# Which queue issues three kinds of stores: az, the normalised z and the projected a, from ScalarE and not from SyncE

## The chip, the core and the metric

The kernel runs on one core of one Trainium2 chip. The metric is the device time of one execution in microseconds. A core has TensorE (PE in the rows; PEld is its weight load), VectorE (DVE), ScalarE (ACT), GpSimd (POOL) and SyncE (SP), which here only issues transfers. A name with a q, as SPq, is an engine's queue of issues.

## What is computed

One decoder layer over 4096 positions of 1024 channels, in float32:

```
h = LN(x)                                        # stored, needed again in unit 3
a_val, a_gate, a_z, b_u, b_v, b_z = split(h @ w_in)        # six of 512 channels
y_a = silu(LN(causal_conv31(a_val * sigmoid(a_gate)))) * silu(a_z)
y_b = gelu(b_u) * (tril(w_s) @ LN(gelu(b_v)) + b_s) * silu(b_z)
h = LN(alpha * h + concat(y_a, y_b) @ w_out)
out = h + sigmoid(h @ w_gate + b_gate) * (p @ w_ple)
```

The convolution is depthwise along the positions, so what it reads, a = a_val * sigmoid(a_gate), is needed with channels on the partitions.

## The kernel before

There are five matrix products with 1024 x 1024 weights, called units: 0 gives a, 1 gives u and v, 2 gives z of both branches (b_z and a_z), 3 is the output projection and 4 the gate. Each unit goes over 16 pairs of 128 positions (`NP`, index p), and for each pair `group` computes a 256 x 1024 product by Strassen-Winograd in seven products of 12 matmuls each (float32 as the sum of two fp32r halves, hi and lo, by three products). The seven go through the PSUM banks pb, pe, pa and pd: ScalarE or VectorE saves pb and pe to pa, s5 (s in the rows), u2 (u) and pd before the next product overwrites or reads them. Those are the evictions of lines 330 to 334. The left operands of the next pair are made meanwhile: `left` copies a tile to ahi on ScalarE and leaves the rest, alo, to VectorE or GpSimd.

Much goes through tensors in DRAM. In unit 0, `a_out` (line 519) transposes a pair's a into the tile at and stores it with four transfers (one for each 128 channels, line 535) to aD, which the convolution reads some pairs later. In unit 2, `body_c` takes silu of az in place and stores it (line 641) to azD; unit 3 loads it again as cz. In unit 3, `z_out` (line 706) normalises a pair's z with one ACTIVATE for each 128 positions (line 716) and stores it (line 717) to zT; unit 4 loads it as zr. Beside this, weights of the next unit are prepared: `combos` loads four quarters (bq, line 183), subtracts them on GpSimd (lines 187 to 196) and stores the seven operands to twD (lines 186 to 197); they come back as wst (line 414) near the end of a unit. Other transfers of this kind are qD (line 251, left operands kept for units 1 and 2, loaded again as qa and qb), hT (493), xr (465), uD, ybD, cD, and hr and y, loads for unit 3.

All transfers are issued by SyncE through the name `dma`. The order on each engine is not the order of the code: a scheduler places all instructions by its own estimate of times, and what an engine is given it runs in that order. Every transfer adds to one of eight semaphores, DMAHW0 to DMAHW7, which the scheduler hands out in turn; a transfer whose semaphore was last used by another waits until that one has landed. An instruction of an engine that waits holds those behind it.

Of the kernel before, what the change touches and what calls it, by code (L numbers as in the profile page):

```python
# [16 lines left out]
P = 128  # L17
# [47 lines left out]
def hybrid_layer_kernel(  # L65
# [16 lines left out]
):  # L82
    nc = tc.nc
    dma = nc.sync.dma_start
    act = nc.scalar.activation
    tt = nc.vector.tensor_tensor
    ptt = nc.gpsimd.tensor_tensor
# [11 lines left out]
    def big(shape, name, dt=F32):  # L99
        return pool.tile(shape, dt, tag="big", name=name, bufs=7)  # L100
# [4 lines left out]
    def utile(shape, name, dt=F32):  # L105
        return pool.tile(shape, dt, tag="u", name=name, bufs=7)
# [4 lines left out]
    def sbank(name):  # L111
        return pbank("S", name, 2)
# [17 lines left out]
    zT = [dram.tile([2, P, D], F32, name=f"zT{p}") for p in range(NP)]  # L130
    qD = [dram.tile([P, 7, C], F32, name=f"qD{p}") for p in range(NP)]
    aD = [dram.tile([CT, P, 2, SB // 2], F32, name=f"aD{b}") for b in range(NS)]
# [3 lines left out]
    azD = [dram.tile([2, P, C], F32, name=f"azD{p}") for p in range(NP)]  # L136
    twD = [None] + [dram.tile([7, P, 4, C], F32, name=f"twD{u}") for u in range(1, 5)]

    def pair(t):
        return t.rearrange("j p d -> p j d")  # L140
# [3 lines left out]
    def moments(halves, mv):  # L144
        st = pool.tile([P, 2, 6], F32, tag="st", name="st", bufs=4)
        for i, h in enumerate(halves):
            nc.vector.bn_stats(st[:, i, :], h)
        nc.vector.bn_aggr(mv, st[:, 0 : len(halves), :])

    def mvtile(n):  # L150
        t = pool.tile([P, 2, 2], F32, tag="mv", name="mv", bufs=6)
        return t[:, 0:n, :]
# [23 lines left out]
    def combos(u):  # L176


        for c in range(4):
            q = big([P, 4, C], "bq")  # L180
            for i in range(2):
                for j in range(2):
                    dma(q[:, 2 * i + j], wq[u, i, j][:, c])
            yield
            for n, k in ((1, 0), (2, 2), (3, 3)):
                dma(twD[u][ROW[n]][:, c], q[:, k])
            ptt(q[:, 0], q[:, 1], q[:, 0], op=SUB)
            dma(twD[u][ROW[5]][:, c], q[:, 0])
            yield
            ptt(q[:, 1], q[:, 3], q[:, 1], op=SUB)  # L190
            dma(twD[u][ROW[7]][:, c], q[:, 1])
            yield
            ptt(q[:, 3], q[:, 3], q[:, 0], op=SUB)
            dma(twD[u][ROW[6]][:, c], q[:, 3])
            yield
            ptt(q[:, 2], q[:, 2], q[:, 3], op=SUB)
            dma(twD[u][ROW[4]][:, c], q[:, 2])
            yield
# [166 lines left out]
    def conv(b, ct):  # L365

        n = SB // 2
        ca = pool.tile([P, 2, HALO + n], F32, tag="ca", name="ca", bufs=2)  # L370
        zy = pool.tile([P, HALO - 1 + n], F32, tag="zy", name="zy", bufs=1)
        if b == 0:
            nc.gpsimd.memset(ca[:, :, 0:HALO], 0.0)
        else:
            dma(ca[:, :, 0:HALO], aD[b - 1][ct][:, :, n - HALO :])
        dma(ca[:, :, HALO:], aD[b][ct])
        e, o = ca[:, 0], ca[:, 1]
        ptt(zy, e[:, 1:], o[:, 0 : HALO - 1 + n], op=SUB)  # L378
        ptt(e, e, o, op=SUB)
        even, odd = (pbank("acc", "acc", 2) for _ in range(2))  # L380
        for k in range(NE):
            w, src = cs_sb[:, ct, k : k + 1], o[:, k : k + n]
            if k == 0:
                nc.vector.tensor_scalar(even, src, w, cb_sb[:, ct : ct + 1], op0=MUL, op1=ADD)
            else:
                stt(even, src, w, even, op0=MUL, op1=ADD)  # L386
            yield
        for k in range(NE):
            if k < NE - 1:
                src = zy[:, k : k + n]  # L390
                dst = src if k == NE - 2 else odd
                stt(dst, src, cw_sb[:, ct, 2 * k + 1 : 2 * k + 2], odd if k else even, op0=MUL, op1=ADD)  # L392
                yield
            src = e[:, k : k + n]
            stt(  # L395
                src if k == NE - 1 else even, src, cw_sb[:, ct, 2 * k : 2 * k + 1], even,
                op0=MUL, op1=ADD,
            )
            yield
        for h, src in ((0, e[:, HALO:]), (1, zy[:, HALO - 1 :])):  # L400
            dma(cD[b][ct][:, :, h], src.rearrange("p (t m) -> p t m", m=P // 2))
        convolved.append((b, ct))
# [15 lines left out]
    def broadcast(src, n, name, tile_of=big):  # L418
        t = tile_of([P, n, src.shape[-1]], name)
        for i in range(n):  # L420
            dma(t[:, i], src[i : i + 1, :].partition_broadcast(P))
        return t
# [95 lines left out]
    def a_out(p, c):  # L518

        at = big([P, CT, 2, P], "at")  # L520
        for j in range(2):
            tp = sbank("ta")
            for ct in range(CT):
                nc.tensor.transpose(
                    out=tp[:, ct * P : (ct + 1) * P], in_=c[j][:, ct * P : (ct + 1) * P],
                    identity=ident,
                )
            act(
                at[:, :, :, j * 64 : (j + 1) * 64],
                tp.rearrange("p (c h m) -> p c h m", c=CT, h=2), ID,  # L530
            )
            yield
        t0 = (p % 4) * P
        for ct in range(CT):
            dma(aD[p // 4][ct][:, :, t0 : t0 + P], at[:, ct])
        if p % 4 == 3:
            for ct in range(CT):
                bg_conv.add(conv(p // 4, ct))
# [88 lines left out]
    def body_c(p, L, W, between):  # L627
        if p == 1:
            bg_w.add(combos(3))
        if p == NP - 3:  # L630
            for i in range(2):
                cgb.append(broadcast(crow[i : i + 1, :], 1, "cgb", utile))
            load_y(0)
        elif p >= NP - 2:
            bg_x.add(y_rows(p - NP + 2))
        ua = big([P, 2, 2, C], "ua")
        us, az = ua[:, 0], ua[:, 1]
        dma(us, pair(uD[p // 2][2 * (p % 2) : 2 * (p % 2) + 2]))
        pa, pd = group(L, W, None, az[:, 0], az[:, 1], between)
        act(az, az, AF.Silu)  # L640
        dma(pair(azD[p]), az)
        for j, ps in ((0, pa), (1, pd)):
            zz = utile([P, C], "zz")
            act(zz, ps, AF.Silu)
            ptt(us[:, j], us[:, j], zz, op=MUL)
        dma(pair(ybD[p]), us)
        if p == NP - 2:
            load_y(1)
        elif p == NP - 1:
            load_h(0)  # L650
            load_y(2)
# [3 lines left out]
    def load_y(p):  # L655
        b, q = p // 4, p % 4
        while (b, CT - 1) not in convolved:
            bg_conv.step(1)
        cz = big([P, 2, 2, C], "cz")
        dma(  # L660
            flat(cz[:, 0]).rearrange("p (c x) -> p c x", c=CT),
            cD[b][:, :, 2 * q : 2 * q + 2].rearrange("c p j h m -> p c (j h m)"),
        )
        dma(cz[:, 1], pair(azD[p]))
        CZ[p] = cz
        Y[p] = big([P, 2, D], "y")
        dma(Y[p][:, :, C:], pair(ybD[p]))

    def y_rows(p):
        cz, y = CZ.pop(p), Y[p]  # L670
        cc = flat(cz[:, 0]).rearrange("p (c j x) -> p c j x", c=CT, j=2)
        for j in (1, 0):
            tp = sbank("tc")
            for ct in range(CT):
                nc.tensor.transpose(
                    out=tp[:, ct * P : (ct + 1) * P],
                    in_=cc[:, ct, j],
                    identity=ident,
                )
            act(y[:, j, 0:C], tp, ID)  # L680
        yield
        mv = mvtile(2)
        for j in (1, 0):
            moments([y[:, j, 0:C]], mv[:, j, :])
        nb = scale_bias(mv)
        yield
        for j in (1, 0):
            ya = y[:, j, 0:C]
            act(ya, ya, ID, scale=mv[:, j, 1:2], bias=nb[:, j : j + 1])
            yield  # L690
            ptt(ya, ya, cgb[0][:, 0], op=MUL)
            ptt(ya, ya, cgb[1][:, 0], op=ADD)
            act(ya, ya, AF.Silu)
            ptt(ya, ya, cz[:, 1, j], op=MUL)
            yield
# [4 lines left out]
    def load_h(p):  # L700
        H[p] = big([P, 2, D], "hr")
        dma(H[p], pair(hT[p]))
# [4 lines left out]
    def z_out(p, z):  # L707
        mv = mvtile(2)
        for j in range(2):
            moments([z[:, j, 0:C], z[:, j, C:]], mv[:, j, :])  # L710
            yield
        nb = scale_bias(mv)
        yield
        yield
        for j in range(2):
            act(z[:, j], z[:, j], ID, scale=mv[:, j, 1:2], bias=nb[:, j : j + 1])
            dma(zT[p][j], z[:, j])
            yield

    def body_d(p, L, W, between):  # L720
# [168 lines left out]
```

## Time and profile before

| | us |
|---|---|
| median of 3 runs | 1897.69 |
| lowest and highest run | 1892.99, 1901.14 |
| the profiled execution | 1898.2 |
| its span, from first to last instruction | 1896.5 |
| TensorE busy in it | 1804.0 |
| VectorE | 1413.6 |
| GpSimd | 1269.9 |
| ScalarE | 892.4 |
| transfers of SyncE's queue, share of 16 DMA engines | 55.3% |

Durations below are from this one profiled execution. Times of day are us from the start of its span. A busy time is the union of an engine's instructions; issues of transfers are not counted as busy. Unit 0 runs to some 430 us, unit 1 to 770, unit 2 to 1080, unit 3 to 1470, unit 4 to the end.

### The profile page before, as it was taken

Reading aid. Unit: us, or ns where it says so; the run is one execution under the profiler, and the core shown is the slowest. Engines: PE = TensorE matmul, PEld = TensorE weight load, DVE = VectorE, ACT = ScalarE, POOL = GpSimd, SP = SyncE. Lnnn points to the kernel's source line nnn. Section 1 sums busy time; section 2 is a strip of 40 time slices with the busy share of each in tenths; the row PEclk is TensorE's granted clock in tenths of the full one; section 3 lists DMA queues with packets and bytes.
Section 4 is the critical chain, followed back from the end, with each engine's and each line's share of the span. In section 5 each row is a group of like instructions: output and inputs, shape, how many; then the busy total and the mean of one; then the engine's idle time right before and its main releaser. Section 6 shows DMA issues by size and latency. Waiting matters only on the chain. (4 is left out here: it accounts for less than half of the span.)

```text
span 1896.5 us, 24392 instructions
## 1 busy us (share of the span) xinstructions
PE 1804.0 (95%) x8322; PEld 1470.9 (78%) x8322; DVE 1413.6 (75%) x2176; ACT 892.4 (47%) x1438; POOL 1269.9 (67%) x1015
## 2 busy tenths in 40 slices
PE   4799999999999999999999899999999999999999
PEld 3687788877788887788888677787887787888887
DVE  8637877797787778978787998887558856665654
ACT  4655555565455555544444634445555422332222
POOL 2878987458777676588668568757676856655541
PEclk9899999999999999999999889999999999999999
DMA  6579776586734445898666758745555322222311
GB/s 239 195 236 359 248 235 206 194 287 211 239 124 147 139 142 173 302 358 298 211 198 227 272 186 284 242 150 191 197 189 220 119 95 78 89 90 95 100 54 52
DMA packets 184940, 363.62 MB, mean 192 GB/s; under 512 B 49648, under 2 KB 74224, under 8 KB 177136
## 3 DMA queue, kind: packets, MB, share of 16 engines
q1 hardware_dynamic: 184816, 362.07, 55.3%
q8 instruction: 66, 1.08, 0.2%
q14 instruction: 58, 0.48, 0.1%
HBM read 211.02 MB, written 150.99 MB: 191 GB/s over the span
## 5 line engine op out<-in xcount | busy, mean ns | idle before, releaser
L232 POOL TENSOR_TENSOR alo<-s,ahi 128x512 fp32r<-128x512 f32 x192 | 262.8, 1382 | 260.7 <-ACT ahi L231 252.9
L312 PE MATMUL pb<-whi,ahi 128*128 128x512 f32 x960 | 385.9, 402 | 18.3 <-ACT pa L330 5.2
L313 PE MATMUL pb<-wlo,ahi 128*128 128x512 f32 x960 | 378.4, 394 | 1.6 <-DVE wlo L173 1.6
L314 PE MATMUL pb<-whi,alo 128*128 128x512 f32 x960 | 378.4, 394 | 0.1
L312 PE MATMUL pe<-whi,ahi 128*128 128x512 f32 x640 | 258.9, 405 | 19.6 <-ACT ahi L231 8.5
L314 PE MATMUL pe<-whi,alo 128*128 128x512 f32 x640 | 256.6, 401 | 2.1 <-POOL alo L232 2.1
L313 PE MATMUL pe<-wlo,ahi 128*128 128x512 f32 x640 | 254.6, 398 | 4.2 <-DVE wlo L173 4.2
L312 PEld LDWEIGHTS pb<-whi,ahi 128*128 128x128 f32 x960 | 182.3, 190 | 63.6 <-ACT pa L330 8.8
L314 PEld LDWEIGHTS pb<-whi,alo 128*128 128x128 f32 x960 | 182.1, 190 | 39.5 <-POOL alo L232 0.6
L313 PEld LDWEIGHTS pb<-wlo,ahi 128*128 128x128 f32 x960 | 182.7, 190 | 38.4 <-DVE wlo L173 2.6
L232 POOL TENSOR_TENSOR alo<-qa,ahi 128x512 fp32r<-128x512 f32 x128 | 171.2, 1353 | 48.1 <-ACT ahi L231 47.8
L231 ACT ACTIVATE ahi<-s 128x512 fp32r<-128x512 f32 x192 | 119.7, 629 | 138.9 <-DVE s L284 54.6
L386 DVE SCALAR_TENSOR_TENSOR acc<-ca,cs_sb,acc 128x512 f32<-128x512 f32 x240 | 180.1, 750 | 4.3
L395 DVE SCALAR_TENSOR_TENSOR acc<-ca,cw_sb,acc 128x512 f32<-128x512 f32 x240 | 179.0, 746 | 0.1
L392 DVE SCALAR_TENSOR_TENSOR acc<-zy,cw_sb,acc 128x512 f32<-128x512 f32 x224 | 166.8, 745 | 1.2 <-POOL zy L378 0.4
L312 PEld LDWEIGHTS pe<-whi,ahi 128*128 128x128 f32 x640 | 122.7, 192 | 47.1 <-ACT ahi L231 10.3
L232 POOL TENSOR_TENSOR alo<-qb,ahi 128x512 fp32r<-128x512 f32 x96 | 126.8, 1329 | 39.2 <-ACT ahi L231 38.2
L313 PEld LDWEIGHTS pe<-wlo,ahi 128*128 128x128 f32 x640 | 122.6, 191 | 30.4 <-DVE wlo L173 6.5
L232 DVE TENSOR_TENSOR alo<-tp,ahi 128x512 fp32r<-128x512 f32 x144 | 98.2, 683 | 62.9 <-ACT ahi L231 60.5
L314 PEld LDWEIGHTS pe<-whi,alo 128*128 128x128 f32 x640 | 122.3, 191 | 27.8 <-POOL alo L232 3.3
L312 PE MATMUL pd<-whi,ahi 128*128 128x512 f32 x320 | 129.4, 404 | 4.4 <-ACT pd L330 3.2
L159 POOL TENSOR_TENSOR mv<-mv,nhalf 128x2 f32<-128x2 f32 (+1 forms) x81 | 55.2, 687 | 111.2 <-DVE mv L158 110.3
(151 smaller groups left out, 4006.7 us busy)
## 6 DMA issues: line engine op xcount, KB each, us to landing
qa<-qD SPq DMA_DIRECT2D x32, 1024.0 KB, 6.5
twD<-bq SPq DMA_DIRECT2D x112, 256.0 KB, 5.7
wst<-twD SPq DMA_DIRECT2D x28, 1024.0 KB, 6.9
qb<-qD SPq DMA_DIRECT2D x32, 768.0 KB, 6.8
xr<-in_x SPq DMA_DIRECT2D x32, 512.0 KB, 5.4
hT<-xr SPq DMA_DIRECT2D x32, 512.0 KB, 3.8
qD<-s SPq DMA_DIRECT2D x64, 256.0 KB, 2.9
bq<-in_wq SPq DMA_DIRECT2D x64, 256.0 KB, 5.2
```

Source lines behind the costliest of these rows:

```text
L159: ptt(mv[:, :, 1], mv[:, :, 1], nhalf[:, 0:n], op=ALU.pow)
L231: act(hi, src, ID)
L232: eng.tensor_tensor(lo, src, hi.bitcast(F32), op=SUB)
L312: nc.tensor.matmul(ps, lhsT=ah[:, k, :], rhs=wh[:, k, :], start=start and k == 0, stop=False, **kw)
L313: nc.tensor.matmul(ps, lhsT=ah[:, k, :], rhs=wl[:, k, :], start=False, stop=False, **kw)
L314: nc.tensor.matmul(ps, lhsT=al[:, k, :], rhs=wh[:, k, :], start=False, stop=k == 3, **kw)
L386: stt(even, src, w, even, op0=MUL, op1=ADD)
L392: stt(dst, src, cw_sb[:, ct, 2 * k + 1 : 2 * k + 2], odd if k else even, op0=MUL, op1=ADD)
L395: stt(src if k == NE - 1 else even, src, cw_sb[:, ct, 2 * k : 2 * k + 1], even, op0=MUL, op1=ADD,)
```

## The change

A second name, `dma_act`, issues from ScalarE's queue, and three of the stores use it. Nothing else in the code differs; the new line shifts all line numbers behind it by one.

```
+    dma_act = nc.scalar.dma_start
...
         for ct in range(CT):
-            dma(aD[p // 4][ct][:, :, t0 : t0 + P], at[:, ct])
+            dma_act(aD[p // 4][ct][:, :, t0 : t0 + P], at[:, ct])
...
         act(az, az, AF.Silu)
-        dma(pair(azD[p]), az)
+        dma_act(pair(azD[p]), az)
...
             act(z[:, j], z[:, j], ID, scale=mv[:, j, 1:2], bias=nb[:, j : j + 1])
-            dma(zT[p][j], z[:, j])
+            dma_act(zT[p][j], z[:, j])
```

The scheduler makes a new order of it. In units 1, 2 and 4 the engines' orders are nearly the same but for the moved stores; in units 0 and 3 all five differ. Three places, with the semaphores for which each row waits (a name of an engine there is that engine's own semaphore).

ScalarE in unit 0 at the third pair, behind the eviction u; c_1001 is the sigmoid of this pair's first half of the gate, s_1143 a left operand of the next pair. Before:

```order
L528 ACTIVATE at<-ta 128x8x64 [waits PE_49]
L549 ACTIVATE c_1001<-c_1001 128x512 [waits DMAHW4_49,DVE_49]
L262 ACTIVATE zq<-tp 128x512 [waits PE_49]
L231 ACTIVATE ahi<-tp 128x512 [waits Pool_49]
L231 ACTIVATE ahi<-s_1143 128x512 [waits DVE_49]
L231 ACTIVATE ahi<-s_1150 128x512 [waits DVE_49,PE_49,Activation_49]
L330 ACTIVATE pd<-pb 128x512 [waits PE_49]
```

and now:

```order
L529 ACTIVATE at<-ta 128x8x64 [waits PE_49]
L536 DMA aD_125<-at 256x1x128 [waits DMAHW5_49,Activation_49]
L263 ACTIVATE zq<-tp 128x512 [waits PE_49]
L232 ACTIVATE ahi<-tp 128x512
L536 DMA aD_125<-at 256x1x128 [waits DMAHW7_49]
L536 DMA aD_125<-at 256x1x128 [waits DMAHW1_49]
L536 DMA aD_125<-at 256x1x128 [waits DMAHW3_49]
L550 ACTIVATE c_1001<-c_1001 128x512 [waits DMAHW4_49,DVE_49]
L232 ACTIVATE ahi<-s_1143 128x512 [waits DVE_49]
L331 ACTIVATE pd<-pb 128x512 [waits PE_49]
```

The four stores of a now stand in ScalarE's order, one behind the second copy to at and three behind the ahi, and the sigmoid and the eviction pd stand behind them. At the fourth pair all four stand in a row behind the ahi, then one ahi and pd.

ScalarE in unit 2 at the second pair, around the store of az; zz is silu of b_z, s_7599 the eviction of pe in the next pair. Before:

```order
L640 ACTIVATE ua<-ua 128x1024 [waits DVE_49]
L644 ACTIVATE zz<-pd 128x512 [waits PE_49]
L330 ACTIVATE s_7599<-pe 128x512
L330 ACTIVATE pa<-pb 128x512 [waits PE_49,Activation_49]
L231 ACTIVATE ahi<-qa 128x512 [waits DMAHW5_49]
```

and now:

```order
L641 ACTIVATE ua<-ua 128x1024 [waits DVE_49]
L642 DMA azD_158<-ua 128x2x512 [waits DMAHW5_49,Activation_49]
L645 ACTIVATE zz<-pd 128x512 [waits PE_49]
L331 ACTIVATE s_7599<-pe 128x512
L331 ACTIVATE pa<-pb 128x512 [waits PE_49]
```

The store of az, whose semaphore was last used by the load of qa, stands between silu of az and zz, and the evictions s and pa behind it.

SyncE in unit 3 at the first pair, where the prepared weights, the loads of cz, y and hr and the stores of z (zT) meet. Before:

```order
L183 DMA bq<-in_wq 128x512 x4
L717 DMA zT_93<-z 128x1024
L660 DMA cz<-cD_130 128x4x256
L717 DMA zT_93<-z 128x1024
L664 DMA cz<-azD_161 128x2x512
L186 DMA twD_176<-bq 128x512 x3
L667 DMA y<-ybD_145 128x2x512
L702 DMA hr<-hT_80 128x2x1024
```

and now:

```order
L184 DMA bq<-in_wq 128x512 x4
L187 DMA twD_176<-bq 128x512
L661 DMA cz<-cD_130 128x4x256
L665 DMA cz<-azD_161 128x2x512
L187 DMA twD_176<-bq 128x512 x2
L668 DMA y<-ybD_145 128x2x512
L703 DMA hr<-hT_80 128x2x1024
```

The two stores of z are gone from SyncE, and the loads of cz do not stand behind them.

## Rows read from the trace of the kernel before

**Rows 1.** The page: each engine's busy us, share of the span, instructions.

```profile
PE 1804.0 (95%) x8322; PEld 1470.9 (78%) x8322; DVE 1413.6 (75%) x2176; ACT 892.4 (47%) x1438; POOL 1269.9 (67%) x1015
```

**Rows 2.** Stretches: length, busy PE, PEld, DVE, ACT, POOL; granted clock, DMA share, GB/s.

```profile
0.00:67.00 67.00, 32.98 (x104) 22.99 (x104) 57.06 (x71) 34.99 (x44) 28.94 (x29) 0.87 0.59 213
...
100.00:430.00 330.00, 321.04 (x1544) 262.44 (x1543) 249.45 (x390) 188.47 (x310) 236.20 (x170) 0.99 0.74 256
...
780.00:1050.00 270.00, 269.44 (x1201) 222.64 (x1200) 219.24 (x325) 123.83 (x211) 211.93 (x173) 1.00 0.79 267
1050.00:1100.00 50.00, 40.19 (x156) 31.49 (x155) 49.87 (x54) 26.39 (x37) 19.63 (x14) 0.83 0.73 262
1100.00:1440.00 340.00, 330.02 (x1599) 269.55 (x1597) 259.18 (x471) 168.91 (x264) 256.48 (x255) 0.99 0.59 203
1440.00:1500.00 60.00, 52.70 (x226) 40.53 (x227) 52.28 (x57) 30.14 (x40) 43.77 (x24) 0.97 0.51 184
```

**Rows 3.** Waits of TensorE, by what ended them: us in total, times, longest.

```profile
PE pb L312 <- ACT pa L330: 5.2, 7, 1.6
...
PE pb L312 <- ACT s L330: 2.0, 1, 2.0
...
PE tc L675 <- DMA cz<-cD: 1.0, 2, 0.5
```

**Rows 4.** The three stores by line: issue min/median/max in ns, first and last.

```profile
L535 SPq DMA_DIRECT2D aD<-at x64: 524/619/1536, 85.4 to 424.0; - x64
...
L641 SPq DMA_DIRECT2D azD<-ua x16: 359/371/872, 780.9 to 1083.7; - x16
...
L717 SPq DMA_DIRECT2D zT<-z x32: 319/332/916, 1135.0 to 1468.9; - x32
```

**Rows 5.** Waits of SyncE's queue: us in total, times, longest.

```profile
SPq L717 <- ACT z L716: 100.1, 23, 16.6
...
SPq L641 <- ACT ua L640: 39.5, 10, 7.4
```

**Rows 6.** Timeline, unit 0's third pair (start, length); the two stores' landing.

```profile
128.68 1.53 SPq L186 DMA_DIRECT2D twD<-bq  x2
...
129.23 0.59 ACT L231 ACTIVATE ahi<-tp 128x512 fp32r<-128x512 f32 x1
...
132.85 0.58 ACT L330 ACTIVATE pd<-pb 128x512 f32<-128x512 f32 x1 [0.36 <-PE pb L314]
...
136.19 0.48 PE L312 MATMUL pd<-whi,ahi 128*128 128x512 f32 x1
...
DMA to landing us min/median/max: 6.7/6.8/6.9
```

**Rows 7.** Timeline, unit 0's fourth pair; landing of the twD store at 156.8.

```profile
154.28 0.59 ACT L231 ACTIVATE ahi<-tp 128x512 fp32r<-128x512 f32 x1
154.29 1.29 POOL L196 TENSOR_TENSOR bq<-bq 128x512 f32<-128x512 f32 x1
...
157.69 0.39 PE L312 MATMUL pd<-whi,ahi 128*128 128x512 f32 x1
...
DMA to landing us min/median/max: 4.1/4.1/4.1
```

**Rows 8.** Timeline, unit 2's second pair; landing of the qa load.

```profile
797.62 0.33 SPq L238 DMA_DIRECT2D qa<-qD  x1
...
799.75 1.05 ACT L640 ACTIVATE ua<-ua 128x1024 f32<-128x1024 f32 x1
...
804.62 0.39 PE L312 MATMUL pe<-whi,ahi 128*128 128x512 f32 x1
...
806.15 0.37 SPq L641 DMA_DIRECT2D azD<-ua  x1
...
DMA to landing us min/median/max: 8.5/8.5/8.5
```

**Rows 9.** Busy time and clock of 5 us in unit 3; columns as rows 2.

```profile
1130.00:1135.00 5.00, 3.55 (x9) 2.87 (x10) 4.39 (x8) 4.42 (x7) 2.73 (x4) 0.68 0.12 29
```

## Prediction

> **What bounds the kernel now.** TensorE. It is busy for 1804.0 us of the span of 1896.5 [rows 1], so at most 92.5 us can be won, and any engine that makes it wait adds its wait to the time. I read the stages next [rows 2]: 34 us of the idle time lie in the first 67 us, before the first of the moved stores; from 100 to 430 us (unit 0, with the stores of a) TensorE idles 9.0 us, from 780 to 1050 (unit 2, stores of az) only 0.6, from 1050 to 1100 9.8, from 1100 to 1440 (unit 3, stores of z) 10.0, from 1440 to 1500 7.3. ScalarE is busy for 188 of the 330 us of unit 0, 57%. Then I asked what TensorE waits for [rows 3]: mostly ScalarE's evictions. Transfers appear with 1.0 us in all, two waits for a cz load. So SyncE's queue hardly holds TensorE, and ScalarE, to which the stores go, is the engine whose delays it feels.
>
> **What moves.** 64 + 16 + 32 = 112 stores leave SyncE and stand in ScalarE's order; the order rows show them there. An issue keeps SyncE for 0.62, 0.37 and 0.33 us in the median, at most 1.54, 0.87 and 0.92 [rows 4]. At the medians that is 64 x 0.62 + 16 x 0.37 + 32 x 0.33 = 56 us of queue time off SyncE and onto ScalarE. No row has a transfer issued by ScalarE; I take SyncE's price, with its medians and maxima as the two ends.
>
> *Plain issue on ScalarE, taken at nothing.* In unit 0 it raises ScalarE from 188 to 188 + 40 = 228 of 330 us, 69%. Four in a row hold it for 2.5 us. What stands behind them is mostly the eviction pd, which at the third pair is done at 132.85 + 0.58 = 133.4 while TensorE's pd product starts at 136.19 [rows 6]: 2.8 us of cover against 2.5. If the cover is gone, a late eviction costs what it costs today, 5.2 us in 7 waits, 0.7 each [rows 3]; 14 of the 16 bursts (without the two below) at 0.7 make the upper end, 10 us.
>
> *The stores' own waits, +8.7 us.* All transfers of the program share eight semaphores, DMAHW0 to 7, in turn; a transfer is not issued until the transfer that last used its semaphore has landed. On SyncE this already happens: the second az store had its source at 799.75 + 1.05 = 800.8, and the store left at 806.15, just when the qa load issued at 797.62 had landed, 8.5 us after its issue [rows 8]. On SyncE that stops loads; on ScalarE, whose instructions run in order, it stops evictions. For each of the 112 stores I set the landing, in the trace of before, of the transfer that holds its semaphore in the changed program against the time at which ScalarE comes to it. Most have landed long before; three places stand out, all where weight preparation (bq, twD) crowds the transfers.
>
> - Third pair of unit 0. ScalarE comes to three stores at 129.23 + 0.59 = 129.8. The last needs a twD store issued at 128.7 and landed 6.7 us later, 135.4 [rows 6]. Then its own issue 0.62 and, by the changed order, a sigmoid, an ahi and the pd eviction, 0.6 each as in rows 6: 137.9. TensorE's pd product starts at 136.19: **1.7 us** of stall.
> - Fourth pair. ScalarE is there at 154.28 + 0.59 = 154.9. The last of the four needs the twD store whose subtraction on GpSimd ends at 155.6; no longer behind four stores of a, it can go at once and lands 4.1 us later, at 159.7 [rows 7]. Issue, ahi and pd eviction end at 161.6; the pd product starts at 157.69: **3.9 us**.
> - Second az store. ScalarE waits from 800.8 to 806.1, then 0.37 for the issue, 0.6 for zz and 0.6 for the eviction s: 807.7. TensorE's pe product, which overwrites what s saves, starts at 804.62 [rows 8]: **3.1 us**.
>
> The lower end of this term is 0 (the semaphores come free earlier since SyncE's order changes too), the upper 12 us, if the first two holds also pass the 2.5 us of bare issue on to TensorE in place of hiding it.
>
> *Given back, -1.9 us.* TensorE's 2.0 us wait for an eviction s in unit 0 [rows 3] comes soon after those two stalls, while GpSimd and VectorE go on working through them; I let it vanish but for 0.1. Bounds 0 and -9.0, unit 0's whole idle time.
>
> *What SyncE's relief brings, -1.0 us.* Loads no longer stand behind SyncE's waits for ScalarE, 100.1 us for z and 39.5 us for az [rows 5]. That is large, but TensorE waits for a transfer only at the two cz loads, 1.0 us [rows 3]; the third place of the order shows cz<-cD behind a store of z before and ahead of it now. The upper end of this gain is the first rival.
>
> *Order.* In units 0 and 3 the scheduler rearranges all engines around the moved stores; in the other units they stand nearly as before. The work is the same and I see no reason for a sign; unit 3's 10.0 us of idle time, either way, bounds it.
>
> **Sum.** 8.7 - 1.9 - 1.0 = +5.8 us. The profiled execution took 1898.2 us, 1.7 more than its span and 0.5 above the median of the runs; 1898.2 + 5.8 = **1904.0 us**.
>
> **Rivals.**
>
> *Faster: SyncE's queue was the hidden cause.* SyncE's 100.1 us of waiting for z [rows 5] also delays loads and the twD stores, and through them buffers, VectorE and ScalarE, so that TensorE's waits bear other names. If half of the idle time of unit 3 and both its borders goes, 27.1 us in rows 2, the time is 1898.2 - 13.5 = 1884.7. For it: the size of SyncE's waits. Against: the waits of rows 3 end on ScalarE, and unit 2, where SyncE waits 39.5 us, keeps TensorE busy for 269.4 of 270. It decides if the idle time at 1050 to 1500 halves. The Trainium skill speaks on both sides here: Perfetto Trace Analysis, DMA Optimizations, suggests one issuing engine for inputs and another for outputs, while DMA: Bandwidth & Descriptors, "Issuing engines are not separate DMA queues", says that another issuing engine only saves issue time on the sequencer. By the second page the gain would be nothing beyond SyncE's 56 us, which no row shows on TensorE's path, so the sum would lack its -1.0; by the first this rival would hold. The rows side with the second, but no run yet shows two issuing engines.
>
> *No change: the holds stay under cover.* If the transfers ahead land some 4 us earlier than in the trace, or TensorE's order has other products to do, nothing of the 8.7 us reaches it and only the cz waits go: 1897.2. For it: at most places the semaphores are free 5 us or more ahead. Against: the az store's wait is seen in the trace itself.
>
> *Slower: the stalls also cost clock.* After the idle time near 1130 us the granted clock of the next 5 us was 0.68 [rows 9]: 3.2 of them at 1.2 GHz and not 2.4, which loses 1.6 us. If each of the three holds is followed by such a fall and nothing is given back, the time is 1898.2 + 8.7 + 3 x 1.6 = 1911.7; with the 10 us of the bursts 1921.7. It decides at a stall of about 2 us: against it, the wait of 2.0 us in unit 0 stands in a stage with a granted clock of 0.99 [rows 2].
>
> **How the numbers follow.** Forecast (holds of 4 to 12 us, 1901 to 1910) 0.43; no change 0.25; faster 0.14; slower 0.18. Range 1888 to 1918: it takes in forecast, no change, most of the slower case and the edge of the faster one. The bound of 0.5% (9.5 us, about what a measurement of this kernel can tell from none) lies at 1888.2 and 1907.2 around the median 1897.69. Faster 0.16: its rival and a little luck of order. Slower 0.32: its rival, and a third of the forecast's spread, where the sum gets beyond 1907. Same 0.52.
>
> **What would show it.** Right: an issue on ScalarE of 0.3 to 0.7 us; ScalarE idle for transfers of 4 to 6 us ahead of the stores near 130, 155 and 800 us, and TensorE's gaps at pd and pe right behind; TensorE busy for some 1804 us as before. The step on SyncE is wrong if unit 3's idle time falls well below 10 us; the step on cover is wrong if TensorE's waits for pa, pd, u or s grow all through unit 0, not at two places. The forecast as a whole is wrong if no idle time on ScalarE ends on a transfer at these three places, or if stretches that I left alone (the borders of the units, 1050 to 1100 above all) move by more than 5 us.

## The result: 10.3 us slower

The changed kernel took 1909.08 us in the median of 12 runs (1899.75 to 1914.79), the kernel before 1898.59 in the median of 12 (1892.99 to 1902.93). The ratio is 1.0054, 95% interval 1.0041 to 1.0067: slower by 10.3 us. That is clear of 1, but the interval lies on both sides of the half per cent that counts as a difference here. Measured once more beside other kernels, in six runs, it was 1.0057 (1.0035 to 1.0078). The forecast of 1904.0 us was 5 us short; the range, 1888 to 1918, held the time.

The profiled execution took 1906.1 us, on the short side of these runs; its span is 1904.4 us, 7.9 more than that of before. All line numbers behind the new definition are one higher: L535, L641 and L717 of before are L536, L642 and L718.

The page's first part, each engine's busy time, beside [rows 1]:

```profile
PE 1804.9 (95%) x8322; PEld 1473.1 (77%) x8322; DVE 1401.4 (74%) x2176; ACT 893.6 (47%) x1438; POOL 1269.2 (67%) x1015
```

TensorE does the same work, 1804.9 us against 1804.0. So 7.0 of the 7.9 us are idle time. The stretches, with the columns of [rows 2]:

```profile
100.00:430.00 330.00, 321.47 (x1554) 264.21 (x1553) 251.12 (x399) 190.25 (x311) 239.66 (x173) 0.99 0.74 257
430.00:780.00 350.00, 334.26 (x1529) 273.96 (x1528) 266.44 (x449) 186.43 (x313) 246.15 (x229) 1.00 0.51 170
780.00:1050.00 270.00, 267.23 (x1190) 220.47 (x1190) 216.31 (x323) 122.83 (x209) 208.89 (x170) 1.00 0.78 264
1050.00:1100.00 50.00, 38.88 (x156) 30.40 (x155) 49.65 (x50) 28.12 (x40) 23.00 (x17) 0.87 0.74 263
1100.00:1440.00 340.00, 327.71 (x1572) 267.11 (x1571) 257.72 (x473) 163.82 (x257) 245.44 (x250) 0.99 0.58 200
1440.00:1500.00 60.00, 54.99 (x237) 43.25 (x236) 49.84 (x57) 35.28 (x47) 44.20 (x25) 0.94 0.57 206
1500.00:1904.40 404.40, 395.35 (x1830) 323.98 (x1828) 236.14 (x328) 111.34 (x187) 205.68 (x109) 0.99 0.24 83
```

and the two of the kernel before that [rows 2] leaves out:

```profile
430.00:780.00 350.00, 336.27 (x1542) 275.91 (x1541) 272.81 (x460) 187.77 (x316) 248.03 (x231) 1.00 0.51 172
1500.00:1896.50 396.50, 388.96 (x1800) 318.24 (x1798) 236.21 (x323) 111.14 (x186) 196.47 (x105) 1.00 0.24 83
```

Unit 0 idles 8.5 us where it idled 9.0, unit 1 15.7 against 13.7, unit 2 2.8 against 0.6, the border behind it 11.1 against 9.8, unit 3 12.3 against 10.0, the next border 5.0 against 7.3, unit 4 with the end 9.1 against 7.5. So the loss is in small pieces, some 2 us each in units 1, 2 and 3 and 1.5 in unit 4; in unit 1 no store has moved. TensorE's waits (us in total, times, longest), beside [rows 3]:

```profile
PE pd L313 <- ACT pd L331: 9.9, 9, 3.6
...
PE tc L676 <- DMA cz<-cD: 6.6, 4, 2.8
PE pb L313 <- ACT pa L331: 6.4, 7, 2.4
...
PE pe L313 <- ACT s L331: 2.9, 2, 2.2
```

The row for pd is in the kernel before

```profile
PE pd L312 <- ACT pd L330: 3.2, 6, 1.3
```

These waits have risen most, by 6.7 us, but hardly by the moved stores: with the new order and all stores on SyncE (e2 below) they are 7.7 us, and in unit 0, where they rose, all idle time together fell. The waits for cz loads have risen from 1.0 to 6.6 us, and there is one new wait of 2.2 us for an eviction s. That one is the second az store, and it can be followed instruction by instruction. First ScalarE, then TensorE (start, length, operation, and in brackets the idle time ahead of it and what ended it):

```profile
800.46 1.05 ACT L641 ACTIVATE ua<-ua 128x1024 f32<-128x1024 f32 x1
806.15 0.38 ACTq L642 DMA_DIRECT2D azD<-ua  x1
806.57 0.60 ACT L645 ACTIVATE zz<-pd 128x512 f32<-128x512 f32 x1 [5.06 <-DMA qa<-qD]
807.07 0.59 ACT L331 ACTIVATE s<-pe 128x512 f32<-128x512 f32 x1
```

```profile
805.11 0.39 PE L315 MATMUL pb<-whi,alo 128*128 128x512 f32 x1
807.71 0.50 PE L313 MATMUL pe<-whi,ahi 128*128 128x512 f32 x1 [2.21 <-ACT s L331]
```

The silu ends at 801.5. ScalarE then stands still until 806.15, when the qa load that holds the store's semaphore has landed; the store, zz and the eviction s follow at their usual prices; s ends at 807.66, and 0.05 us later TensorE starts the product that overwrites its source. In [rows 8] the same wait sat on SyncE and cost nothing.

### The profile page after: what moved, and what is told of

It reads as the page before. It is cut to its first block, busy times and chain, and to the rows that moved or that the text cites. A ratio compares the mean times of both kernels' runs of the same rounds, so it can differ in the third digit from the quotient of the medians.

```text
span 1904.4 us, 24332 instructions
## 1 busy us (share of the span) xinstructions
PE 1804.9 (95%) x8322; PEld 1473.1 (77%) x8322; DVE 1401.4 (74%) x2176; ACT 893.6 (47%) x1438; POOL 1269.2 (67%) x1015
## 4 chain that ended last, share of the span: by engine, by line
PE 66%; DMA 10%; DVE 10%; POOL 6%; issue 5%; ACT 3%; SPq 0%; ACTq 0%; POOLq 0%; DVEq 0%
PE pb L313 8%; PE pb L314 8%; PE pb L315 8%; PE pe L315 6%; PE pe L313 5%; PE pe L314 5%; PE pp L806 4%; PE pd L313 3%; PE tp L258 3%; PE pd L315 3%; PE pa L313 3%; PE pd L314 3%; PE pa L314 3%; PE pa L315 3%; POOL alo L233 3%
## 5 line engine op out<-in xcount | busy, mean ns | idle before, releaser
L315 PEld LDWEIGHTS pb<-whi,alo 128*128 128x128 f32 x960 | 182.5, 190 | 39.3
```

The source lines that it names most:

```text
L315: nc.tensor.matmul(ps, lhsT=al[:, k, :], rhs=wh[:, k, :], start=False, stop=k == 3, **kw)
```

## Experiments

**How the order was held.** The scheduler lays out all engines anew when a store changes its queue, so the change is two things at once: another queue and another order. To take them apart, the program is built twice. The first build only yields the order of its instructions; in the second, each instruction is tied behind its neighbour on its own engine, by an edge that sets the order and adds no wait. The names in parentheses are the kinds of store that ScalarE issues.

```
-    nc = _bacc.Bacc( ... )
+    def build(on_act, names=None):
...
+            if names:
+                by, last = {i.name: i for i in nc.cur_bb.bb.instructions}, {}
+                for i in (by[k] for k in names if k in by):
+                    if i.engine in last:
+                        tc.add_manual_dep(i, last[i.engine], info, reason="pinned")
+                    last[i.engine] = i.name
...
+    nc, feed = build(('a', 'az', 'z'), names_of(build(())[0]))
```

So TensorE, VectorE and GpSimd run one of two streams, "old" (of before) or "new" (of the changed kernel), and only the stores stand in one queue or the other. The traces bear this out: in e1, e3 and e4 all 8322 matmuls, 2176 instructions of VectorE and 1438 of ScalarE come in the sequence of before, in e2 and e5 to e9 in that of the changed kernel. The table has all runs. "Gap" is TensorE's idle time at the second az store, "cz" its waits for cz loads from 1100 us on, both from the one profiled execution of each kernel; "clock" is the mean granted clock over all timed runs of the kernel, and "lost" the mean of a run's time times (1 - clock). e3, e6 and e11 have 2.0, 0.6 and 2.0 us more of cz waits ahead of 1100 us, where no store of z has gone yet; they are not counted. e5 has 6 runs, e9 9, the others 12. The runs of before beside e1 to e4 had 0.9871 and 24.4 us, beside e5 to e8 0.9872 and 24.3, beside e9 to e12 0.9875 and 23.8. "us" is the ratio less one times 1898. A half-width of 0.0015 is 3 us, so a difference between two rows is uncertain by about 4 us, and most rows are not clear of one another; e10, the kernel before against itself, strays by 1 us.

| run | order | on ScalarE | ratio (95%) | us | gap | cz | clock | lost |
|---|---|---|---|---|---|---|---|---|
| changed | new | a, az, z | 1.0054 (1.0041 to 1.0067) | +10.3 | 2.21 | 6.6 | 0.9850 | 28.6 |
| e5 | new | a, az, z | 1.0057 (1.0035 to 1.0078) | +10.8 | 2.48 | 6.1 | 0.9853 | 28.0 |
| e1 | old | a, az, z | 1.0014 (0.9996 to 1.0031) | +2.7 | 2.22 | 6.9 | 0.9864 | 25.8 |
| e2 | new | none | 1.0011 (1.0000 to 1.0023) | +2.1 | 0 | 2.7 | 0.9856 | 27.4 |
| e3 | old | az | 1.0008 (0.9995 to 1.0022) | +1.5 | 2.08 | 2.5 | 0.9873 | 24.1 |
| e4 | old | z | 0.9994 (0.9980 to 1.0008) | -1.1 | 0 | 5.4 | 0.9868 | 25.0 |
| e6 | new | az | 1.0028 (1.0012 to 1.0045) | +5.3 | 2.28 | 3.3 | 0.9872 | 24.3 |
| e7 | new | a | 1.0019 (1.0005 to 1.0034) | +3.6 | 0 | 3.4 | 0.9868 | 25.0 |
| e8 | new | z | 1.0016 (1.0002 to 1.0031) | +3.0 | 0 | 5.4 | 0.9865 | 25.7 |
| e9 | new | all but the second az | 1.0030 (1.0013 to 1.0048) | +5.7 | 0 | 6.0 | 0.9861 | 26.4 |
| e10 | old | none (before) | 1.0005 (0.9991 to 1.0018) | +0.9 | 0 | 3.5 | 0.9869 | 24.8 |
| e11 | mixed | none | 1.0001 (0.9987 to 1.0015) | +0.2 | 0 | 3.3 | 0.9876 | 23.5 |
| e12 | mixed | az but the second, z | 1.0007 (0.9994 to 1.0021) | +1.3 | 0 | 6.6 | 0.9867 | 25.3 |

### e1 and e2: queue or order

The edit of e1 is the diff above; e2 swaps the two lists:

```
-    nc, feed = build(('a', 'az', 'z'), names_of(build(())[0]))
+    nc, feed = build((), names_of(build(('a', 'az', 'z'))[0]))
```

> All three kinds of store go to ScalarE's queue as in the changed kernel, but every instruction of every engine keeps the place it has in the kernel before; the stores stand in ScalarE's stream where the old program's overall order puts them. The theory after the first result: the 10.3 us have two sources, holds of ScalarE at a store that waits for an earlier transfer (TensorE gap of 2.21 us at 805.5 and 0.76 us at 158.2 in the changed kernel's trace, up to about 3 us more at 134), and the new order in which the scheduler lays the work out (cz waits of 6.6 us against 1.0, larger gaps at the borders of the units). By it this kernel pays the holds alone: 3 to 6 us above before, and the cz waits stay near 1 us. Rival Q, the second queue by itself (its transfers crowd those of SyncE): about 10 us above, with cz waits of 5 us or more. Rival O, the order by itself: 0, within 1 us.

> The mirror image: every engine's instructions stand in the order of the changed kernel, but the three kinds of store are issued by SyncE. By the theory of two sources it pays the order alone: 4 to 7 us above before, no gap of 2 us near 805, cz waits of about 6 us. Rival Q: 0, within 1 us, cz waits back at about 1 us. Rival O: 10 us above, the whole loss.

Neither alone makes the loss: 2.7 us for the queue in the old order, 2.1 for the new order with the old queue, where the theory wanted 3 to 6 and 4 to 7. Rival O, the order alone, is out by e2's upper end, 1.0023; rival Q in its time, about 10 us, by e1's, 1.0031. But one of Q's marks came up: the cz waits follow the queue and not the order, 6.9 us in e1 and 2.7 in e2, the reverse of what the theory of two sources had. The sum is 4.8 of 10.3 us, and 5.5 us are in neither.

### e3 and e4: two kinds of store, in the old order

```
-    nc, feed = build(('a', 'az', 'z'), names_of(build(())[0]))
+    nc, feed = build(('az',), names_of(build(())[0]))      (e3)
+    nc, feed = build(('z',), names_of(build(())[0]))       (e4)
```

> Order of the kernel before; only the sixteen stores of az go from ScalarE. By the theory of two sources 2 to 4 us above before, and the whole of it one TensorE gap near 805 us, where the second az store waits for a load of SyncE that lands at 806.1 us. Rival Q: 0 to 1 us (no crowding in that unit). Rival O: 0.

> Order of the kernel before; only the thirty-two stores of the third unit's turned z go from ScalarE. By the theory of two sources 0, within 1 us, since none of them reaches ScalarE before the transfer that it has to wait for has landed. Rival Q: 4 to 6 us above, as cz waits of about 6 us. Rival O: 0. If SyncE's freed queue sends the cz loads earlier, as the prediction had it, up to 1 us below.

The az stores bring the gap near 805 us, 2.08 us of it, and 1.5 us of time, under the 2 to 4 expected and not clear of nothing. The z stores bring the cz waits, 5.4 us, as rival Q had it, but no time: 0.9994, where Q wanted 4 to 6 us. How a z store delays a cz load is seen at one place, the third pair of unit 3, in e10 (stores on SyncE) and e4 (on ScalarE), both in the old order. SyncE's queue in e10, and TensorE's wait there:

```profile
1158.81 1.46 SPq L717 DMA_DIRECT2D zT<-z  x2
1160.36 2.32 SPq L183 DMA_DIRECT2D bq<-in_wq  x4
1163.37 0.38 SPq L660 DMA_DIRECT2D cz<-cD  x1
```

```profile
1169.47 0.63 PE L675 MATMUL tc<-ident,cz 128*128 128x128 f32 x4 [1.88 <-DMA cz<-cD]
```

The same in e4, and behind it one row of SyncE's waits in the 15 us from 1150:

```profile
1154.04 2.50 SPq L184 DMA_DIRECT2D bq<-in_wq  x4
1159.90 0.38 SPq L661 DMA_DIRECT2D cz<-cD  x1
```

```profile
1165.34 1.09 PE L676 MATMUL tc<-ident,cz 128*128 128x128 f32 x4 [3.38 <-DMA cz<-cD]
```

```profile
SPq L661 <- DMA zT<-z: 3.2, 1, 3.2
```

In e10 the two stores go first, then four weight loads, and the cz load 0.7 us behind the last. In e4 the weight loads end 3.4 us before the cz load, and the cz load is stopped for 3.2 us until a z store has landed: the semaphores are shared, so a store that leaves SyncE's queue can still stop SyncE.

### e5 to e8: the changed kernel again, and each kind of store in the new order

e5 is the changed kernel itself. The others:

```
+    nc, feed = build(('az',), names_of(build(('a', 'az', 'z'))[0]))      (e6)
+    nc, feed = build(('a',), names_of(build(('a', 'az', 'z'))[0]))       (e7)
+    nc, feed = build(('z',), names_of(build(('a', 'az', 'z'))[0]))       (e8)
```

> The changed kernel once more, word for word, beside the other kernels of this set. Its first measurement stood 10.3 us above before; the queue in the old order cost 2.7 us (e1) and the new order with SyncE's queue 2.1 us (e2), which leaves 5.5 us that neither shows. If the two work together, in that the gaps that they leave push TensorE's granted clock down more often (mean granted clock 0.9850 in the twelve first runs of the changed kernel, against 0.9871 in the 35 runs of before), it comes out at 9 to 11 us above before again, with a mean clock near 0.985. If the first figure was high by chance or by the place where it was taken, 4 to 6 us above.

> Order of the changed kernel; only the sixteen stores of az go from ScalarE, the others from SyncE. By the theory of two sources: the 2.1 us of e2 and the hold near 805 us, whose step between the first and the third pair of that unit was 2.4 to 2.5 us in the three traces that have it: 4 to 5 us above before, or up to 7 if the gap also costs clock. If the loss comes from another of the three stores: 2 us, as e2.

> Order of the changed kernel; only the 64 stores of the projected a go from ScalarE. By the theory of two sources 2 to 4 us above before (e2 and the 0.76 us gap at 158). If it is these stores that meet the new order badly, at the border of the first two units where the changed kernel's clock fell a second time (0.71 at 440 us, 1.00 there in e2): 5 to 8 us above.

> Order of the changed kernel; only the 32 stores of z go from ScalarE. By the theory of two sources 1 to 3 us above before, as e2, since in the old order the same edit gave 0.9994 (e4). If these stores meet the new order badly (cz loads that land late behind them, 6.6 us of waits in the changed kernel's trace against 2.2 us in one wait in e2's): 5 to 8 us above.

The 10.3 us were no accident: 10.8, and a mean clock of 0.9853. e5 lies in the range expected if queue and order work together, e6 to e8 in those of the theory of two sources. On top of e2's 2.1 us the az stores bring 3.2, those of a 1.5, those of z 0.9. That sums to 7.7, and what is missing to 10.3 is within the error. So in the new order the parts may add up, and the az stores are the largest by their figure, though not clear of the others. In e6's trace the gap also cost clock. Its 5-us slices from 800, with the columns of [rows 2]:

```profile
800.00:805.00 5.00, 2.72 (x12) 1.95 (x12) 5.00 (x9) 1.38 (x3) 0.71 (x1) 1.00 1.01 410
805.00:810.00 5.00, 5.00 (x16) 3.98 (x16) 1.06 (x2) 1.88 (x4) 3.15 (x4) 0.66 1.05 368
810.00:815.00 5.00, 5.00 (x24) 4.14 (x23) 1.88 (x3) 1.47 (x3) 5.00 (x5) 1.00 1.02 320
```

Behind 2.28 us of idleness the clock is 0.66 for a slice: 1.7 us lost, 16 matmuls done instead of 24. In the other four traces with the gap it stayed at 1.00, and over its twelve runs e6 lost no more clock than before (24.3 us both), so this fall is not what makes e6 slower.

### e9: one store of 112 put back

```
-        dma_of('az')(pair(azD[p]), az)
+        dma_of('az2' if p == 1 else 'az')(pair(azD[p]), az)
...
+    nc, feed = build(('a', 'az', 'z'), names_of(build(('a', 'az', 'az2', 'z'))[0]))
```

> The changed kernel in its own order, with one of its 112 moved stores, that of the second az, back on SyncE. The theory has its hold as the largest single piece: the step between the first and the third pair of that unit (2.5 us in the changed kernel) goes to 0, nothing else moves, and the time falls by 2.5 us, or by about 4 where the gap also made the clock fall: 6 to 8 us above before, against 10.3 and 10.9 for the changed kernel. If a wait takes its place (SyncE held by the same semaphore, or the next store held instead), 10 us above as before.

5.7 us above before, a little under the 6 to 8 expected, against 10.3 and 10.8 with that store on ScalarE. The intervals just overlap (1.0013 to 1.0048 and 1.0041 to 1.0067), so the size, 4.6 and 5.1 us with an error of some 4 to 5, is loose, and the gap of 2.2 to 2.5 us explains half of it; the place is not, since the gap is in all five traces that have this store on ScalarE and in none of the other nine, the two of before among them. In e9, ScalarE and then SyncE at the place:

```profile
796.15 1.05 ACT L641 ACTIVATE ua<-ua 128x1024 f32<-128x1024 f32 x1
798.50 0.60 ACT L645 ACTIVATE zz<-pd 128x512 f32<-128x512 f32 x1 [1.30 <-PE pd L315]
799.00 0.59 ACT L331 ACTIVATE s<-pe 128x512 f32<-128x512 f32 x1
```

```profile
801.85 0.37 SPq L642 DMA_DIRECT2D azD<-ua  x1
```

```profile
780.00:1050.00 270.00, 269.44 (x1200) 222.79 (x1199) 218.99 (x324) 124.32 (x211) 212.47 (x173) 1.00 0.78 268
```

zz and s run 1.3 and 1.8 us behind the silu, the store waits in SyncE's queue until 801.85, and TensorE is busy for 269.44 of unit 2's 270 us, to the digit what [rows 2] has. In this unit no wait took the place of the one removed.

### e10 to e12: before again, and two mixed orders

e10 is the kernel before. The other two take the new order for the first unit and half of the second, and the old one behind it:

```
+    new, old = names_of(build(('a', 'az', 'az2', 'z'))[0]), names_of(build(())[0])
+    head = new[: new.index(MARKS[24]) + 1]
+    kept = set(head)
+    nc, feed = build((), head + [k for k in old if k not in kept])               (e11)
+    nc, feed = build(('az', 'z'), head + [k for k in old if k not in kept])      (e12)
```

> The kernel before, once more, as if it were a change: how far a ratio of two equal kernels strays, and a second trace of it. Expected within 2 us of before. Of the trace: the stretch from the second to the sixth pair of the fourth unit was 1 to 4 us shorter in the first trace of before than in the three other kernels with the same order; if that was chance, the cz waits here are 2 to 5 us against the 1.0 us there.

> All stores on SyncE; the first unit and half of the second in the order of the changed kernel, everything behind that in the order of before. The traces of the six kernels in the new order are 3 us shorter, on average, than the four in the old one from the fifth to the last pair of the first unit, and 2 to 3 us longer early in the fourth unit. If both are the order's, this kernel keeps the gain alone: 2 to 4 us below before. If the gain is given back at the border to the second unit: 0, within 1 us.

> The mixed order of e11, with the stores of az, but for the second, and of z on ScalarE, and those of the projected a on SyncE: what the runs so far leave as the best combination. By sums: e11's 2 to 4 us below before, 1.5 us less for az without its hold (1.5 measured in e3, of which 2.5 were the hold), 1 us less for z (e4): 3 to 6 us below before. If the queues only cost: at or above e11.

The second trace of before has 3.5 us of cz waits: the 1.0 us of [rows 3] was a lucky execution. Over the fourteen traces the two sets now stand apart, whatever the order: with z on SyncE 1.0 to 3.5 us, mean 2.8, with z on ScalarE 5.4 to 6.9, mean 6.1.

The first of these waits, for the second pair near 1145 us, goes by the order all the same. It is 1.96 to 2.61 us in the seven traces in the new order, with z on either queue, and 0.18 to 2.05 in the other seven; and behind it the granted clock falls to the level of 0.50, 1.2 GHz, for some us in all of the first seven and in none of the others. In e2, with no store on ScalarE:

```profile
1142.14 1.94 PE L676 MATMUL tc<-ident,cz 128*128 128x128 f32 x8 [2.23 <-DMA cz<-cD]
```

```profile
1140.00:1145.00 5.00, 2.86 (x11) 2.70 (x12) 2.38 (x5) 1.19 (x2) 2.95 (x3) 0.67 1.06 382
```

So one wait and one fall of the clock come with the new order, whoever issues the stores. Neither mixed order beats the kernel before; the 3 us that single traces showed in unit 0 don't show in e11's time, and e12 is 1.1 us above e11. Both missed the 2 to 6 us of gain that their expectations put first: in e11 nothing is left of it, and in e12 the stores on ScalarE add nothing but cost, if anything. Nothing here is worth keeping.

## Why the prediction was right or wrong

**Right: the engine, the price, the kind of cause.** TensorE's busy time did not move, and the one hold that is shown is ScalarE's. An issue costs ScalarE what it cost SyncE [rows 4] (ns, min/median/max; first and last start):

```profile
L536 ACTq DMA_DIRECT2D aD<-at x64: 520/632/1597, 85.7 to 421.0; - x64
...
L642 ACTq DMA_DIRECT2D azD<-ua x16: 366/366/442, 781.2 to 1087.4; - x16
...
L718 ACTq DMA_DIRECT2D zT<-z x32: 326/326/1317, 1138.0 to 1476.1; - x32
```

That plain issue hides is borne out as far as the runs go: the a stores cost 1.5 us in e7 against e2, uncertain by 4, where the bursts' upper end was 10.

One reading behind the choice of the engine was wrong. The waits of TensorE in the view of [rows 3] add up to 87.4 us, and ScalarE's evictions end 10.6 of them, not most; VectorE ends 48.1.

**Right: the second az store.** The step said that the eviction s would end at 807.7 us and TensorE lose 3.1. It ended at 807.66, and TensorE lost 2.21, because its place in the program comes 0.9 us later there. This is the one hold that e9 proves by taking it away.

**Wrong: the third and fourth pair, +5.6 us.** ScalarE does stop there. In the changed kernel, third and fourth pair:

```profile
131.61 3.21 ACTq L536 DMA_DIRECT2D aD<-at  x3
134.92 0.63 ACT L550 ACTIVATE c<-c 128x512 f32<-128x512 f32 x1 [3.49 <-DMA aD<-at]
...
135.98 0.58 ACT L331 ACTIVATE pd<-pb 128x512 f32<-128x512 f32 x1
```

```profile
155.21 2.53 ACTq L536 DMA_DIRECT2D aD<-at  x3
157.79 0.63 ACT L232 ACTIVATE ahi<-s 128x512 fp32r<-128x512 f32 x1 [2.20 <-DMA aD<-at]
158.32 0.58 ACT L331 ACTIVATE pd<-pb 128x512 f32<-128x512 f32 x1
```

The pd eviction ends at 136.56 and 158.90, against the 137.9 and 161.6 forecast from old landings; TensorE's pd products start at 136.61 with no gap of 0.1 us ahead and at 158.96 behind one of 0.76. In e1, in the very order of before, there is no gap at either place. The step took landings from the trace of before, and in the changed kernel the last store could go 1.1 and 2.6 us sooner; the text had this in its lower bound and in the "no change" rival, for everything but the az store. 0.8 us in place of 5.6.

**Wrong: what is given back, -1.9 us.** In e1, in the old order, TensorE's idle time from 182.5 us is 2.05, against 2.0 in [rows 3]: the stalls that were to swallow it hardly exist. In the changed kernel it is gone, but by the order: a wait of 1.39 us for pd stands near the place, and one of 1.43 in e2 as well. Unit 0 idles 0.4 us less in all.

**Wrong in sign: SyncE's relief, -1.0 us.** The cz waits rose, by 3.3 us on average (6.1 against 2.8). Of SyncE's 100.1 us of waiting for z [rows 5] some 62 only moved on to the cz loads, first before, then now:

```profile
SPq L660 <- DVE pd L334: 44.3, 8, 18.2
...
SPq L661 <- DVE pd L335: 106.4, 8, 18.1
```

The argument compared the order of issues and took the landing for granted. This was also the ground of the faster rival; its test, that the idle time of 1050 to 1500 us halve, failed: 28.4 us against 27.1. Of the two pages of the Trainium skill that the prediction named there, Perfetto Trace Analysis, DMA Optimizations, with one engine for inputs and another for outputs as a thing that may help, is not borne out here (0.9994 in e4, 1.0054 with all three stores); DMA: Bandwidth & Descriptors, "Issuing engines are not separate DMA queues", by which only issue time is saved, agrees with the time of e4, 0.9994 (0.9980 to 1.0008).

**Mis-sized: order, taken at 0.** e2 gives 2.1 us, 0 to 4.4. The bound "unit 3's idle time, either way" held.

**Left out: the clock.** The forecast put the stalls' clock at nothing and left it to the rival at 1911.7 us, to which the measured 1909.08 is nearer than to 1904.0. Time times granted clock is the time that a run would have taken at full clock, if TensorE had work all through the slow stretches. It is 1879.8 us on average for the changed kernel and 1880.2 for e5, against 1873.7 and 1873.6 for before beside e1 and e5: +6.1 and +6.6, each uncertain by some 2 us. The rest, some 4 us, is the lost column, 28.6 and 28.0 against 24.4 and 24.3. So the 5.8 us of stalls forecast are about what is left without the clock, but by errors that cancel: 2.2 + 0.8 + 0 + 3.3 = 6.3, if the cz waits count in full, where the sum had 3.1 + 5.6 - 1.9 - 1.0. That is luck, and even the 6.3 is not the idle time of the trace, where unit 0 has less of it than before and units 1 and 4 have 2.0 and 1.5 us more, for which the sum has no term. The 4 to 5 us that the forecast lacks are, by this reading, the clock's.

The rival had the right price for a fall (1.6 us; 1.7 in e6). Its reason against was misread: 0.99 is an average over 330 us, and in the trace of before the slice right behind the wait of 2.0 us shows the fall:

```profile
185.00:190.00 5.00, 5.00 (x15) 3.59 (x16) 5.00 (x9) 2.51 (x5) 5.00 (x3) 0.66 1.04 404
```

Its places were mostly wrong: behind the holds the clock fell in one trace of five at the az store and in none at the other two. The falls behind the first 100 us come after the cz wait near 1145 us (above) and, as in the kernel before, near 1130 us [rows 9] and at the borders: between units 0 and 1 both traces lose 3.4 us. Whether a fall comes at one and the same wait varies. In the changed kernel's trace, part of this border is

```profile
435.00:440.00 5.00, 3.01 (x12) 2.18 (x12) 2.59 (x4) 3.64 (x7) 1.03 (x1) 1.00 0.91 311
440.00:445.00 5.00, 4.00 (x12) 3.15 (x13) 0.00 (x0) 2.00 (x4) 3.97 (x4) 0.71 0.12 39
```

and in e2's, with the same TensorE stream and as long a wait ahead (2.45 us in both),

```profile
435.00:440.00 5.00, 2.55 (x12) 1.80 (x11) 2.54 (x4) 3.64 (x7) 2.29 (x2) 1.00 0.80 293
440.00:445.00 5.00, 5.00 (x23) 4.09 (x23) 1.45 (x3) 2.90 (x6) 3.76 (x4) 1.00 0.01 3
```

The two profiled executions, at mean clocks of 0.986 (before) and 0.985, hardly differ in the clock. The split of 6 and 4 us is read off the clocks of all runs; no run holds the clock fixed, so it is not shown by experiment, and why one border falls and the other doesn't stays open.

**Open, too.** The cz waits are longer in every trace with z on ScalarE, by 3.3 us on average, yet the time is -1.1 (e4 less before), +0.9 (e8 less e2) and +1.1 us (e12 less e11). Their mean is 0.3: either the waits don't reach the end or the error hides them. Unit 3's idle time from 1100 to 1440 us is 12.7 us on average in the seven traces with z on ScalarE and 11.3 in the other seven, so more than half of the 3.3 us comes out of other waits there. And e1, which has both the gap and the cz waits, costs 2.7 us, at most 5.9: the old order takes the same stores more lightly than the new one, by an amount (10.3 - 2.7 - 2.1 = 5.5 us) that is hardly larger than its error of about 4.6. Whether queue and order really work on each other isn't settled.

## What to carry to other kernels

Before a transfer moves to a compute engine's queue, look at what it will wait for there besides its own data: one store of 112, stopped for 4.6 us by an unrelated load, made some 5 of the 10.3 us, give or take 4, and putting that one back is the cheap repair of that part. A queue that is relieved of a store isn't free of it, since landings and shared semaphores bind the two queues: take every landing of the old trace as a guess, with its own bound. Where a scheduler decides the order, hold the order fixed to price an edit, and ask many executions rather than one trace. And an average of the clock over a long stage hides single falls: read it in short slices.

## What was unexpected of the hardware

The clock sets a part of the spread. The kernel before, 35 times in one set, ran at mean granted clocks between 0.984 and 0.990 (about 11 us of lost time between them) and at 1890.8 to 1905.1 us. But the lost time accounts for only 40% of the variance of these times, and for 11% and 18% in the two other sets of before. The single falls looked at all cost about the same: 1.7 us in e6's slice at 0.66, 1.6 in the slice at 0.68 of [rows 9], 1.5 at 0.71 in the border above. And one trace is a draw: two executions of the same program had 1.0 and 3.5 us of cz waits.
